# Merge units of the self-attention stage: fixed places in TensorE's order, lower planner rank, part of their vector work on GpSimd

## The chip, the cores and the metric

The kernel runs on one core of a Trainium2 chip. A core has a matrix engine (TensorE; PE in the profile, PEld for its weight loads), a vector engine (VectorE, DVE), a scalar engine (ScalarE, ACT), a general engine (GpSimd, POOL) and SyncE (SP), which here only issues DMAs. The metric is device time in microseconds (us); a median of several runs is given.

## The reference

One inference step of a one-layer encoder over 1024 prompt tokens and 8 x 16 sample tokens (together T = 1152), width 1024, all in float32. The input u is normalised and projected by `w_in`; three branches follow, and their results are merged:

```python
A: o_a = diff_attn(q, k, v) * silu(g_a)        # 8 heads, chunk-causal mask + ALiBi bias
B: o_b = rg_lru(conv(x_r)) * silu(g_b)
C: o_c = cross_attention(q_m, 256 memory tokens) * silu(g_c)
p = einsum('btnw,nwd->btnd', stack([o_a, o_b, o_c]), w_branch)
m = sum_n sigmoid(g_merge_n) * p_n
x = LayerNorm(alpha * x + m @ w_o)

# differential attention, per head: two score matrices over the halves of q and k
s1 = q1 k1^T * scale + bias;  s2 = q2 k2^T * scale + bias
w  = softmax(s1) - lam * softmax(s2)
o  = w @ v;  o = o * rsqrt(mean(o*o) + eps) * subln_g * lam_scale
```

The merge is a matrix product of 1152 x 1024 by 1024 x 1024 for each of the three branches, weighted by a gate and added up.

## The kernel before

**Precision.** Products that need nearly full float32 run as three passes: each operand is split into a high half (a cast on ScalarE, line 134) and a low half (the value minus its high half, on VectorE, line 131); `mm3` issues high x high, high x low, low x high.

**Stages ("windows").** After the projections come `wkg` (recurrent branch B and most of the projections), then `wkc` (cross-attention of the prompt), `wkx` (cross-attention of the samples), `wka` (self-attention of the prompt: this is where most of the change lies, from about 1330 to 1656 us), `wks` (self-attention of the samples), then the output product and the last LayerNorm.

**Merge units.** While an attention stage runs, the merge product of a branch that is already done is used as fill work for TensorE. `m_units(i, e)` gives, for branch i and the block e of 128 output columns, three units, one for each third of the 1152 tokens (384). A unit (`units_for`) loads its gate slice `gmr` (line 271) and, if branches went before, the sum so far `mr` (line 274), both through SP; issues 24 matmuls into a PSUM bank `pj`; then VectorE computes (gate + 1) x product (line 278) and adds the sum so far (line 283); SP stores the result to `d_m` (line 284). The first unit of a block starts the weight load `xr` two blocks ahead; the first two units of a block split the next block's weights in two parts (`w_split`: cast to `xh`, low half to `xl`).

**Self-attention, per head h.** `tload` loads a bias table into `th` (one buffer) and GpSimd scales it for the head (line 313). `qk` makes the high half of the two query halves and the masked copies (`Q`, lines 324 and 325), loads the raw keys and splits them (`K`, lines 134 and 131); Q and K have one buffer each, and the raw keys take the buffers that the raw queries leave. For each block i of 128 queries, `s1` issues the scores `sc` of both halves (i+1 key blocks), VectorE adds the table and takes the minimum (line 366, 16 such instructions a head), ScalarE takes the exponential (line 369), and VectorE combines the two softmaxes (line 376). `s2` transposes the weights (TensorE, line 387; ScalarE copies, line 389), `s3` multiplies by v. The step i of `s1` is followed by `s2` and `s3` of i-2; what is left after `s1` of i = 7 is `tail`: `s2` and `s3` of 6 and 7, `s4a` (the norm; its square root on ScalarE) and `s4b` (transpose, gate, store).

**What sets the order.** Each engine works through its own instruction stream in order. A planner makes the streams when the kernel is built: it follows the program with estimated durations and gives each engine, of the instructions that are ready by its estimate, the one that stands earliest in the program. So a merge unit that stands late in the program is issued early wherever an engine would stand idle. `seq` (lines 426 to 444) is the program order: three units ahead of head 0, then two in each of the 8 heads, the first behind the `s1` of i = 5 with its `s2` and `s3` of 3, the second inside `tail`, which stands behind `qk` of the next head:

```python
seq += at[:18] + [F[2 * h]] + at[18:]
seq += [lambda h=h: (qk(h + 1), tload(h + 1), vload(h + 1))] + tail[:3] + [F[2 * h + 1]] + tail[3:]
```

**Cross-attention of the prompt, start.** `setup` (line 453) loads the 256 x 1024 memory keys with one DMA into `mr`, stores them to an output, and `qget` loads the queries; `mk_tr` transposes the keys by blocks of 256 columns.

## Time and profile before

| | us |
|---|---|
| median of 3 runs | 2013.34 (2007.81 to 2016.94) |
| profiled execution, its own time | 2009.19 |
| its span | 2006.8 |
| TensorE busy | 1929.4 |
| VectorE busy | 1275.0 |
| ScalarE busy | 951.4 |
| GpSimd busy | 118.1 |

Matmuls overlap one another, so a busy TensorE need not be at its peak. The granted clock is a share of TensorE's full speed. The chain that ended last lies for 86% of the span on TensorE, 5% on VectorE, 4% on DMA and 3% on ScalarE. "Idle before" in a row is the time in which the engine stood still ahead of that instruction, with what ended it.

### The profile page before, as it was taken

The numbers are of one execution on the slowest core, as the hardware profiler recorded it, in microseconds if no ns is written. First come the engines' busy times: TensorE is split into PE (matmuls) and PEld (weight loads), VectorE is DVE, ScalarE is ACT, GpSimd is POOL, SyncE is SP. The second block draws the span as 40 slices with busy tenths as digits, with TensorE's granted clock in tenths as the row PEclk, the third lists the DMA queues.
The fourth block names the chain that finished last, engine by engine and source line by source line (L and its number), as shares of the span: only waits on it lengthen the run. The fifth ranks groups of instructions, "written<-read, shape, count | busy, mean of one in ns | idle before, by whom it ended". The sixth has DMA issues, their size and how long they took to land.

```text
span 2006.8 us, 35547 instructions
## 1 busy us (share of the span) xinstructions
PE 1929.4 (96%) x13880; PEld 1792.8 (89%) x13880; DVE 1275.0 (64%) x2402; ACT 951.4 (47%) x2035; POOL 118.1 (6%) x186
## 2 busy tenths in 40 slices
PE   7999999999999999999999899999998778999998
PEld 7999999999999999999999888878997666677986
DVE  7746776655655575756545464459998764444688
ACT  5433333445545555655445432338877763323310
POOL 2100000000000000000000001000110001110000
PEclk9999999999999999999999999999998889999999
DMA  8756333343443343333424856978676418777952
GB/s 272 239 159 178 120 102 111 114 139 126 137 146 118 130 128 118 110 125 122 151 96 147 269 187 219 309 241 248 195 207 176 116 39 266 257 253 247 296 159 94
DMA packets 314151, 344.58 MB, mean 172 GB/s; under 512 B 19124, under 2 KB 262196, under 8 KB 313984
## 3 DMA queue, kind: packets, MB, share of 16 engines
q1 hardware_dynamic: 313984, 342.32, 54.1%
q8 instruction: 109, 1.79, 0.4%
q14 instruction: 58, 0.48, 0.1%
HBM read 241.45 MB, written 100.81 MB: 171 GB/s over the span
## 4 chain that ended last, share of the span: by engine, by line
PE 86%; DVE 5%; DMA 4%; ACT 3%; issue 1%; SPq 1%; POOL 0%; DVEq 0%; ACTq 0%
PE pj L138 23%; PE ba L1026 15%; PE bb L1026 14%; PE bc L1026 14%; PE sc L138 6%; PE o L138 4%; PE tr L387 1%; PE tr L601 1%; PE tr L138 1%; PE pv L138 1%; DMA ocr<-d_oT 1%; PE tr L415 1%; PE tr L743 1%; DVE p L366 1%; DMA d_oT<-oc 1%
## 5 line engine op out<-in xcount | busy, mean ns | idle before, releaser
L138 PE MATMUL pj<-uhi,xh 128*128 128x384 f32 x576 | 200.1, 347 | 0.9 <-DVE gmr L278 0.7
L138 PE MATMUL pj<-ulo,xh 128*128 128x384 f32 x576 | 197.9, 344 | 1.0 <-DVE ulo L131 1.0
L138 PE MATMUL pj<-uhi,xl 128*128 128x384 f32 x576 | 197.5, 343 | 0.0
L134 ACT CAST xh<-xr 128x512 fp32r<-128x512 f32 x124 | 74.4, 621 | 104.5 <-PE pj L138 50.1
L138 PEld LDWEIGHTS pj<-ulo,xh 128*128 128x128 f32 x576 | 108.8, 189 | 10.8 <-issue 8.2
L138 PEld LDWEIGHTS pj<-uhi,xh 128*128 128x128 f32 x576 | 108.8, 189 | 10.7 <-issue 5.8
L138 PE MATMUL sc<-K,Q 128*128 128x512 f32 (+4 forms) x384 | 107.7, 391 | 7.3 <-ACT K L134 2.8
L138 PEld LDWEIGHTS pj<-uhi,xl 128*128 128x128 f32 x576 | 108.7, 189 | 5.3 <-issue 4.6
L369 ACT ACTIVATE p<-p,sst 128x256 f32<-128x256 f32 (+6 forms) x128 | 100.6, 788 | 21.1 <-DVE sst L366 20.4
L138 PE MATMUL pj<-w,uhi 128*128 128x256 f32 x576 | 106.9, 286 | 0.5 <-ACT uhi L134 0.2
L366 DVE CUSTOM_DVE_ANT_0 p<-sc,th 128x256 f32<-128x256 f32 (+6 forms) x128 | 98.3, 769 | 12.7 <-PE sc L138 9.8
L138 PE MATMUL pj<-wo,mh 128*128 128x512 f32 x432 | 98.7, 390 | 0.3 <-ACT wo L134 0.3
L131 DVE TENSOR_TENSOR xh<-s,xh 128x512 fp32r<-128x512 f32 x80 | 55.1, 689 | 66.7 <-ACT xh L134 65.6
L138 PEld LDWEIGHTS pj<-wo,mh 128*128 128x128 f32 x432 | 80.8, 188 | 18.0 <-ACT wo L134 1.0
L131 DVE TENSOR_TENSOR xl<-s,xl 128x512 fp32r<-128x512 f32 x80 | 55.2, 690 | 61.7 <-ACT xl L134 60.5
L138 PEld LDWEIGHTS pj<-w,uhi 128*128 128x128 f32 x576 | 90.8, 193 | 1.6 <-ACT uhi L134 0.7
L1026 PE MATMUL ba<-uhi,xh 128*128 128x288 f32 x432 | 91.0, 296 | 0.4 <-DVE go L1041 0.4
L1026 PE MATMUL ba<-uhi,xl 128*128 128x288 f32 x432 | 90.7, 295 | 0.0
L1026 PE MATMUL bb<-uhi,xl 128*128 128x288 f32 x432 | 90.7, 296 | 0.0
L1026 PE MATMUL bc<-uhi,xh 128*128 128x288 f32 x432 | 90.7, 295 | 0.0
L1026 PE MATMUL bc<-uhi,xl 128*128 128x288 f32 x416 | 87.8, 296 | 0.0
L1026 PE MATMUL bb<-uhi,xh 128*128 128x288 f32 x416 | 87.7, 296 | 0.0
(319 smaller groups left out, 5132.8 us busy)
## 6 DMA issues: line engine op xcount, KB each, us to landing
xr<-in_w_in_dram SPq DMA_DIRECT2D x82, 512.0 KB, 4.8
xr<-in_w_branch_dram SPq DMA_DIRECT2D x32, 512.0 KB, 5.1
ck<-in_cache_k_dram SPq DMA_DIRECT2D x32, 512.0 KB, 6.9
cv<-in_cache_v_dram SPq DMA_DIRECT2D x16, 1024.0 KB, 5.9
d_gm<-go SPq DMA_DIRECT2D x24, 576.0 KB, 3.3
gmr<-d_gm SPq DMA_DIRECT2D x72, 192.0 KB, 4.2
d_m<-gmr SPq DMA_DIRECT2D x64, 192.0 KB, 2.4
mr<-d_m SPq DMA_DIRECT2D x48, 192.0 KB, 4.9
```

Of the source, the lines that this page charges most:

```text
L131: V.tensor_tensor(out, a, b, OP.subtract)
L134: SC.copy(hi, src)
L138: PE.matmul(out, a, b, start=start, stop=stop)
L366: V.tensor_tensor_reduce(s[:, :L].rearrange("p (a b) -> p a b", a=nb), ps[z][:, :nb, :w], X["th"][:, 896 - 128 * i:896 - 128 * i + L].rear ...
L369: SC.activation(s[:, :L], s[:, :L], AF.Exp, scale=-1.0, bias=st_[:, z, i:i + 1], accum_out=st_[:, 2 + z, i:i + 1])
L387: PE.transpose(t[:, 128 * j:128 * j + 128], X["w", h, i][:, 128 * k:128 * k + 128], ident)
L415: PE.transpose(t[:, 128 * j:128 * j + 128], X["ob", h][:, 4 * g + j, :], ident)
L601: PE.transpose(t[:, 128 * j:128 * j + 128], X["ck", n, s // 2][:, j, 128 * (s % 2):128 * (s % 2) + 128], ident)
L743: PE.transpose(t[:, 256 * d + 128 * m:256 * d + 128 * m + 128], X["k", b][:, m, c:c + 128], ident)
L1026: PE.matmul(t, w[:, p, k, :], m[v][:, k, a], start=first and k == 0 and y == 0, stop=last and k == 3 and y == 2, skip_group_check=True)
```

## The change

- The 18 units of branch C in the self-attention stage (`m_units(2, e)`, e = 1 to 6) get `eng=GP`: their sum (line 283) and the weight low halves of the block that follows (`w_split`) move from VectorE to GpSimd.
- `mm` returns its instruction; `s1` keeps the last score matmul in `X["at"]`. `behind(f)` builds a unit within `tc.issue_after`: its TensorE instructions get an ordering edge that puts them behind that matmul in TensorE's stream (an order, not a wait for it to finish). Other engines' instructions get no edge.
- `first(fs)` builds the attention steps `at` and `tail` within `tc.high_priority(100)`: the planner ranks them as if they stood 100 instructions earlier. `qk`, `tload`, `vload`, `gload` and the units are not in it.
- The first unit of a head moves from behind `at[:18]` to behind `at[:15]`, which ends with `s1` of i = 5; the second from behind `tail[:3]` (in the last head `tail[:6]`) to behind `tail[:1]`.
- In `s4a` one 128 x 8 product moves from VectorE to a Square on ScalarE.
- `setup` of the prompt's cross-attention loads the memory keys with four DMAs of 256 columns each.

```diff
-    def split(hi, lo, src):
+    def split(hi, lo, src, eng=None):
         SC.copy(hi, src)
-        sub(lo, src, raw(hi))
+        (eng or V).tensor_tensor(lo, src, raw(hi), OP.subtract)
 
     def mm(out, a, b, start, stop):
-        PE.matmul(out, a, b, start=start, stop=stop)
+        return PE.matmul(out, a, b, start=start, stop=stop)
...
-    def w_split(i, part):
+    def w_split(i, part, eng=None):
...
-        split(wt[i][0][:, a], wt[i][1][:, a], wr[i][:, a])
+        split(wt[i][0][:, a], wt[i][1][:, a], wr[i][:, a], eng)
...
             for p in range(2):
                 if str(p) in do:
-                    w_split(i + 1, p)
+                    w_split(i + 1, p, eng)
...
             if more:
-                V.tensor_tensor(g, x["m"], g, OP.add)
+                (eng or V).tensor_tensor(g, x["m"], g, OP.add)
             SY.dma_start(d_m[e][:, TC * c:TC * c + TC], g)
...
-                        mm(t[:, b, :w], q, X["K"][z][y][:, w * b:w * b + w], y == 0, y == 1)
+                        X["at"] = mm(t[:, b, :w], q, X["K"][z][y][:, w * b:w * b + w], y == 0, y == 1)
...
-            V.scalar_tensor_tensor(d, z1, EPS, z1, op0=OP.mult, op1=OP.mult)
+            SC.activation(d, z1, AF.Square, scale=EPS ** 0.5)
...
         for e in range(1, 7):
-            F += m_units(2, e)
+            F += m_units(2, e, eng=GP)
+
+        def behind(f):
+            def go():
+                with tc.issue_after(X["at"].ins):
+                    f()
+            return go
+
+        def first(fs):
+            def go(f):
+                with tc.high_priority(100):
+                    f()
+            return [lambda f=f: go(f) for f in fs]
...
-            seq += at[:18] + [F[2 * h]] + at[18:]
+            at, tail = first(at), first(tail)
+            seq += at[:15] + [behind(F[2 * h])] + at[15:]
             if h < 7:
-                seq += [lambda h=h: (qk(h + 1), tload(h + 1), vload(h + 1))] + tail[:3] + [F[2 * h + 1]] + tail[3:]
+                seq += [lambda h=h: (qk(h + 1), tload(h + 1), vload(h + 1))] + tail[:1] + [behind(F[2 * h + 1])] + tail[1:]
                 seq.append(lambda h=h: gload(h + 1))
             else:
-                seq += tail[:6] + [F[15]] + tail[6:]
+                seq += tail[:1] + [behind(F[15])] + tail[1:]
...
-            SY.dma_start(mr, d_kv[:, 0:D].rearrange("(a p) d -> p a d", p=128))
+            for j in range(4):
+                c = slice(256 * j, 256 * j + 256)
+                SY.dma_start(mr[:, :, c], d_kv[:, c].rearrange("(a p) d -> p a d", p=128))
```

## Rows read from the trace of the kernel before

**Rows 1.** The page: busy us (share) and instructions; granted clock in 40 slices.
```profile
PE 1929.4 (96%) x13880; PEld 1792.8 (89%) x13880; DVE 1275.0 (64%) x2402; ACT 951.4 (47%) x2035; POOL 118.1 (6%) x186
PEclk9999999999999999999999999999998889999999
```

**Rows 2.** Scaling of the head's table on GpSimd, seven of eight: start, duration, idle before.
```profile
1378.90 4.41 POOL L313 TENSOR_SCALAR th<-th 128x1152 f32<-128x1152 f32 x1 [40.90 <-DMA th<-in_c_tab_dram]
1414.80 4.81 POOL L313 TENSOR_SCALAR th<-th 128x1152 f32<-128x1152 f32 x1 [31.48 <-DMA th<-in_c_tab_dram]
...
1524.80 3.44 POOL L313 TENSOR_SCALAR th<-th 128x1152 f32<-128x1152 f32 x1 [29.79 <-DMA th<-in_c_tab_dram]
1566.11 4.21 POOL L313 TENSOR_SCALAR th<-th 128x1152 f32<-128x1152 f32 x1 [37.87 <-DMA th<-in_c_tab_dram]
1604.84 4.22 POOL L313 TENSOR_SCALAR th<-th 128x1152 f32<-128x1152 f32 x1 [34.52 <-DMA th<-in_c_tab_dram]
```

**Rows 3.** Stretches: length, busy of PE, PEld, DVE, ACT, POOL; clock, DMA share, GB/s.
```profile
1387.10:1410.70 23.60, 23.60 (x149) 21.32 (x149) 22.64 (x66) 20.48 (x56) 0.00 (x0) 1.00 0.72 208
1410.70:1423.30 12.60, 12.60 (x95) 12.16 (x93) 11.37 (x17) 8.63 (x23) 4.81 (x1) 1.00 0.69 190
1576.90:1600.60 23.70, 20.12 (x102) 15.46 (x102) 20.92 (x60) 18.88 (x54) 0.00 (x0) 0.86 0.39 111
1600.60:1614.10 13.50, 9.33 (x63) 8.67 (x63) 7.94 (x14) 9.45 (x23) 4.22 (x1) 0.87 0.44 122
1638.20:1656.10 17.90, 10.58 (x71) 9.33 (x72) 6.74 (x15) 7.20 (x21) 0.00 (x0) 0.84 0.04 15
1660.00:1680.00 20.00, 15.92 (x96) 12.25 (x95) 7.98 (x16) 5.00 (x8) 3.69 (x16) 1.00 1.01 325
```

**Rows 4.** Stretches, instructions on the merge units' bank alone: PE, PEld, DVE, ACT.
```profile
1387.10:1410.70 23.60, 10.93 (x47) 7.94 (x47) 1.08 (x2) 0.00 (x0) 1.00 0.72 208
1410.70:1423.30 12.60, 6.42 (x33) 5.18 (x31) 0.54 (x1) 0.00 (x0) 1.00 0.69 190
1351.20:1524.80 173.60, 76.77 (x351) 59.69 (x349) 8.64 (x16) 0.00 (x0) 1.00 0.75 213
```

**Rows 5.** VectorE in order of time, from one head to the next, with fill.
```profile
1416.54 0.54 DVE L278 SCALAR_TENSOR_TENSOR gmr<-gmr,pj 128x384 f32<-128x384 f32 x1
1417.12 2.67 DVE L283 TENSOR_TENSOR gmr<-mr,gmr 128x384 f32<-128x384 f32 x1
...
1422.06 1.23 DVE L131 TENSOR_TENSOR K<-qr,K 128x1024 fp32r<-128x1024 f32 x1 [1.14 <-ACT K L134]
...
1423.28 0.42 DVE L366 CUSTOM_DVE_ANT_0 p<-sc,th 128x256 f32<-128x256 f32 x1
...
1424.11 0.55 DVE L278 SCALAR_TENSOR_TENSOR gmr<-gmr,pj 128x384 f32<-128x384 f32 x1
```

**Rows 6.** VectorE in order of time, from head 6 to head 7, without fill.
```profile
1612.75 1.23 DVE L131 TENSOR_TENSOR K<-qr,K 128x1024 fp32r<-128x1024 f32 x1 [2.21 <-ACT K L134]
```

**Rows 7.** Groups of VectorE and GpSimd: count, busy us, mean ns, idle before.
```profile
L283 DVE TENSOR_TENSOR gmr<-mr,gmr 128x384 f32<-128x384 f32 x21 | 13.6, 648 | 0.1
L278 DVE SCALAR_TENSOR_TENSOR gmr<-gmr,pj 128x384 f32<-128x384 f32 x21 | 11.4, 543 | 9.0 <-PE pj L138 9.0
L131 DVE TENSOR_TENSOR xl<-xr,xh 128x512 fp32r<-128x512 f32 x14 | 9.4, 681 | 0.0
L955 POOL TENSOR_TENSOR rt<-ra 128x576 f32<-128x576 f32 x16 | 19.2, 1198 | 542.5 <-DVE rc L954 542.5
L1164 POOL TENSOR_TENSOR w<-wr,w 128x512 fp32r<-128x512 f32 x12 | 18.0, 1506 | 53.7 <-ACT w L1162 53.7
```

**Rows 8.** SP's queue: start, issue time, line, transfers.
```profile
1412.22 4.32 SPq L318 DMA_DIRECT2D qr<-d_k  x4
```

**Rows 9.** TensorE and ScalarE, start of the prompt's cross-attention.
```profile
1119.45 0.66 PE L465 MATMUL tr<-ident,mr 128*128 128x128 f32 x4 [3.30 <-DMA mr<-d_kv]
...
1123.19 2.01 ACT L486 ACTIVATE qm<-qr 128x1024 fp32r<-128x1024 f32 x2
```

More of the change, by code (lines that the diff above doesn't have):

```diff
@@ L239, in w_split, with units_for @@
         a = slice(4 * part, 4 * part + 4)
-        split(wt[i][0][:, a], wt[i][1][:, a], wr[i][:, a])
+        split(wt[i][0][:, a], wt[i][1][:, a], wr[i][:, a], eng)
     PLANS = {"a": {0: "L"}, "b": {1: "L0", 2: "1"}, "": {0: "L0", 1: "1"}, "s": {2: "L01"}}
-    def units_for(col, ev, w, pre, cs=(0, 1, 2), plan=""):
+    def units_for(col, ev, w, pre, cs=(0, 1, 2), plan="", eng=None):
         i = len(order)
@@ L264, in body, with m_units @@
     gq_ = [None]
-    def m_units(i, e, put=None, cs=(0, 1, 2), plan=""):
+    def m_units(i, e, put=None, cs=(0, 1, 2), plan="", eng=None):
         x = {}
@@ L282, in ev @@
             if more:
-                V.tensor_tensor(g, x["m"], g, OP.add)
+                (eng or V).tensor_tensor(g, x["m"], g, OP.add)
             SY.dma_start(d_m[e][:, TC * c:TC * c + TC], g)
-        return units_for(128 * e, ev, w_br[i], pre, cs, plan)
+        return units_for(128 * e, ev, w_br[i], pre, cs, plan, eng)
     def swap(wk, i, ps, bufs):
```

## The prediction

> **What bounds the kernel now.** The page comes first: TensorE is busy for 96% of the span at full clock, except in the 31st to 33rd of 40 slices, where the granted clock falls [rows 1]. A slice is 50.2 us, so the fall lies near 1505 to 1656 us: the second half of the self-attention stage. Everything else that the change touches there is read from this stage, not from the 96%.
>
> The stage has a clock of its own: the table scaled on GpSimd once a head. From 1378.90 to 1524.80 four heads pass, 36.5 us each; the next two take 41.3 and 38.7 us, and the last needs 51.3 us from its scaling at 1604.84 to the end of the stage at 1656.1 [rows 2, 3]. So heads got slower although nothing was added to them. The stretches say why. A head falls into a score phase (from the first to the last of the sixteen line-366 instructions) and a boundary (from there to the first of the next head). [...] The merge units make the difference: 16 of them (the line-278 count) ran between 1351.2 and 1524.8 in 76.77 us of TensorE, 4.8 us each, about 3.3 a head [rows 4]. The program places two a head; the planner spent them early, and the last three heads had none.
>
> The early and the bare heads differ by only 2 to 5 us, so TensorE is not the only bound. Without units an early head holds 23.60 - 10.93 = 12.7 us of TensorE in its score phase and 12.60 - 6.42 = 6.2 us in the boundary [rows 3, 4]. VectorE holds 20.9 us in the bare score phase of 23.7 [rows 3]: nearly the phase. The boundary is a chain: the last scores free Q, ScalarE and VectorE make the next Q, that frees the buffers for the raw keys, their DMAs go out at 1412.22 [rows 8], ScalarE casts, VectorE makes the low half at 1422.06, and the next line 366 starts at 1423.28, as that ends [rows 5]. The low half waited 1.14 us for ScalarE; in a bare boundary 2.21 [rows 5, 6].
>
> **The change part by part.** *Units behind given scores.* Two a head, 2 x 4.8 = 9.6 us of TensorE, one in the score phase and one in the boundary. TensorE then holds 12.7 + 4.8 = 17.5 us in the score phase and 6.2 + 4.8 = 11.0 in the boundary, below both lengths. The edge orders one engine's stream and adds no wait at run time; queued behind a unit are attention matmuls, and the lower rank lets ready ones go between. The clock: 51% of a bare head is real TensorE work at full clock ((12.7 + 6.2) / 37.2), and there it falls; at (17.5 + 11.0) / 35.2 = 81% I take 1.00, as the stretch at 1660 us had with 15.92 of 20 us busy [rows 3]. If it falls there too, the phase goes back to the bare 23.7.
>
> *Score phase.* VectorE's bare 20.9, plus one line 278 of 0.54 [rows 7], plus port waits (below) 0.4, plus the 1.0 us that it idled in a filled phase (23.60 - 22.64, [rows 3]): 22.9 us. Bounds: 21.9 with no idle time, 23.7 as now.
>
> *Boundary.* 12.6 with fill; one low half of 0.68 [rows 7] leaves VectorE's queue ahead of Q, port waits add 0.4: 12.3 us. Bounds: 11.9, and 13.5 as in a bare one [rows 3]. The lower rank of `qk` against `tail` puts copies of `tail` ahead of Q and K on ScalarE; that cost is inside the upper bound, since ScalarE already makes the key's low half wait 2.21 there [rows 6]. A head: 35.2 us, bounds 33.8 to 37.2.
>
> *Work moved to GpSimd.* A head loses two sums of 0.65 and 1.33 low halves of 0.68 on VectorE, 2.2 us [rows 7]. On GpSimd no row shows these shapes in this stage; the nearest are 1.51 us for a 128x512 low half and 1.20 for a 128x576 product, which by size gives 0.80 for a sum [rows 7]: 2 x 0.80 + 1.33 x 1.51 = 3.6 us a head. GpSimd has room, 4.81 of 36 us being used [rows 2]. But the two engines disturb each other: the sum at 1417.12 took 2.67 us instead of 0.65, and ended at 1419.79, just after GpSimd's table scaling (1414.80 + 4.81 = 1419.61) [rows 2, 5]. So a VectorE operation with two operands from SBUF can wait for a GpSimd operation that has begun. The wait is between nothing and the whole 3.6 us; I take 0.8 a head (0.4 in each part), nearer the lower end, since at these durations most starts miss each other.
> [...]
>
> *Queues passed.* The store of a unit now waits on SP for GpSimd instead of VectorE. Behind it stand the raw keys of the next head if the planner puts them there: 0 to 4.81 us (one table scaling, [rows 2]); I take 0, since the keys go out at 1412.22 and the boundary's unit is only read at 1416.54 [rows 5, 8]. On POOL the table scaling can stand behind a unit's sum: the second rival below the forecast.
>
> *Small edits.* The Square takes one 128x8 instruction from VectorE to ScalarE, out of 60 or more in a phase: 0, within 0.2 us either way. The memory keys in four pieces: TensorE waited 3.30 us for the whole load [rows 9] and can start a transpose on the first quarter, but the scores behind need the queries, which ScalarE only converts at 1123.19 [rows 9], and three more DMA issues stand ahead of the queries' load. Bounds -3.3 and +3.2 (three issues at 4.32/4 = 1.1, [rows 8]); I take -1, a third of the wait, as the queries come late anyway.
>
> *Sum.* The four early heads: 4 x (36.5 - 35.2) = 5.2. The two bare ones: 41.3 + 38.7 - 70.4 = 9.6. The last: score phase 23.7 to 22.9, and its end of 17.9 at clock 0.84 [rows 3] to some 16 at full clock: 2.7. Start of head 0: 0, its load on VectorE being the least. Keys: 1. Together 18.5; 2009.19 - 18.5 = 1990.7, so **1991 us**. The profiled execution lies 4.2 below the median and inside the runs shown, so I leave the number as it is.
>
> **Rivals.** *Full overlap (1973 us).* If the chains hide, the head is set by the busiest engine: VectorE 20.9 + 7.9 + 1.1 = 29.9, TensorE 28.5 [rows 3, 4], with 10% of waits 33 us. That gives 4 x 3.5 + (80 - 66) + 7 for the last head (the mean gain of a bare one) + 1 = 36. For it: every engine is then near 30. Against it: the boundary's DMA chain is not touched.
> *Port (2013 us, no change).* GpSimd's 3.6 us a head all fall on VectorE's path: 2.8 more than taken, times 8 is 22. For it: the 2.67. Against it: only some VectorE operations read two SBUF operands; line 278, whose product is in PSUM, took its 0.54 us at 1416.54 in the midst of the scaling [rows 2, 5].
> *Table behind the sum (2026 us, slower).* Place: POOL's in-order stream in the boundary. The scaling ends at 1419.61, 3.7 us before the line 366 that needs it [rows 2, 5]. If the sum of the boundary's unit stands ahead of it, the scaling starts only when that unit is done. It decides from the point where the unit's line 278 starts later than 1423.28 - 4.81 - 0.80 - 0.54 = 1417.1; today two start at 1416.54 and 1424.11 [rows 5], one on each side. At 1424.11 the table would be ready at 1430.3, 7 us late; 5 us, between on time and that, over 7 boundaries is 35 against the gain: 1991 + 35 = 2026. Against it: the planner would have to expect the unit earlier than the table's DMA.
>
> **How the numbers follow.** What a measurement of this kernel can tell from no change is about 0.5%, 10 us: faster is below 2003. Forecast 0.52, own range 1979 (head 33.8) to 2008 (head 37.2): 0.45 faster, 0.07 same. Full overlap 0.13, faster. Port 0.19: 0.02 faster, 0.14 same, 0.03 slower. Table 0.16: 0.04 same, 0.12 slower. So faster 0.60, same 0.25, slower 0.15. The range 1970 to 2018 leaves out the far end of the full overlap and most of the table's case.
>
> **What would show it.** Right: line-278 instructions come two a head to the end of the stage; the granted clock stays near 1.00 from 1520 to 1640; the eight scalings lie 34 to 36 us apart. Wrong: scalings 37 us or more apart with the clock at 1.00 (the chain or the port); line 376 or the key's low half well above their durations (port); a table scaling that waits for a merge sum, and line 366 for it (table); the clock falling in each boundary.

## The result, and the profile after

The changed kernel takes 2032.99 us (median of 6 runs, 2028.46 to 2038.63) against 2013.96 for the kernel before in the same runs (6 runs, 2007.81 to 2021.10): a ratio of 1.0097 (95% interval 1.0069 to 1.0125). It is slower, by 19 us; 18.5 us of gain were forecast, and the time lies outside the range. (Every ratio below is against the kernel before on the same chip in the same rounds of runs; it is not made from the medians and can differ a little from theirs.)

The profiled execution took 2032.9 us, its span is 2031.1, 24.3 us longer than that of before, whose execution was one of the quicker ones. The page of the changed kernel, the lines that answer to [rows 1]:

```profile
PE 1937.6 (95%) x13880; PEld 1799.9 (89%) x13880; DVE 1272.8 (63%) x2364; ACT 954.2 (47%) x2043; POOL 148.7 (7%) x216
...
PEclk9999999999999999999999899989898998999999
```

Four things that the change was to do, it did. The 18 sums and 12 low halves ran on GpSimd (its busy time rose by 30.6 us). Units came two a head up to the end of the stage (line-278 counts 1, 2, 2, 2, 2, 2, 2, 3 from head 0 to head 7; before 3, 3, 4, 3, 3, 0, 0, 0). The clock no longer falls in one block of slices, but a little in many. And the heads became even. They became evenly slow: GpSimd's scaling of the table, to be held against [rows 2], now three of the eight.

```profile
1424.73 3.27 POOL L313 TENSOR_SCALAR th<-th 128x1152 f32<-128x1152 f32 x1 [22.20 <-DMA th<-in_c_tab_dram]
...
1466.50 3.57 POOL L313 TENSOR_SCALAR th<-th 128x1152 f32<-128x1152 f32 x1 [22.66 <-DMA th<-in_c_tab_dram]
...
1505.35 3.72 POOL L313 TENSOR_SCALAR th<-th 128x1152 f32<-128x1152 f32 x1 [23.29 <-DMA th<-in_c_tab_dram]
```

From the second scaling to the last (1386.84 to 1625.34) a head takes 39.75 us; from 1378.90 to 1604.84 it took 37.66 before [rows 2].

**Where the 24.3 us came in**, read by landmarks of the two traces. The first scores of the stage start 4.2 us later (1349.4 to 1353.6). The last line 366 pair of head 0 is 7.5 late. Over the next seven heads 14.8 more come in, 2.1 a head, and that pair of head 7 is 22.2 late. The end of the stage is 21.4 late, and the first transpose of the next window 25.0 (1670.4 to 1695.4). From there on the lag stays. So some 15 of the 24 us are the length of heads 1 to 7, about 3 more that of head 0, and the rest lies ahead of the first scores and behind the last head.

**Which part of a head grew.** The prediction's boundary between heads (first line 366 of a head) is no good mark any more: block 0's scores now start before the second key is ready, so that "boundary" shrank from 12.6 to 9.1 us while the "score phase" grew from 23.6 to 29.9 or 33.0. A mark that holds in both kernels is the start of line 366 for block i = 3, where all of K, the table and the buffers of the head before are there. From block 3 to block 7 (the *late part*) a head took 12.7 us before and takes 14.9 now; from block 7 to block 3 of the next head (the *turn*) 25.1 before, 24.9 now (means of seven). Stretches of before and then of after, with the columns of [rows 3]: the late part and the turn of one head, and the seven heads as a whole.

```profile
1432.20:1444.90 12.70, 12.70 (x84) 12.02 (x83) 11.65 (x32) 10.69 (x33) 0.00 (x0) 1.00 0.81 241
1444.90:1469.40 24.50, 24.26 (x168) 22.75 (x166) 21.81 (x51) 18.90 (x46) 4.55 (x1) 1.00 0.70 189
1371.52:1635.60 264.08, 240.93 (x1476) 213.14 (x1475) 227.25 (x524) 203.46 (x532) 32.10 (x7) 0.92 0.60 169
```

```profile
1444.00:1460.00 16.00, 15.18 (x78) 13.61 (x79) 12.77 (x31) 12.22 (x35) 0.00 (x0) 0.81 0.45 132
1460.00:1483.90 23.90, 20.05 (x137) 17.51 (x135) 19.21 (x39) 16.32 (x42) 5.58 (x3) 1.00 0.65 175
1378.97:1657.84 278.87, 244.23 (x1481) 215.67 (x1480) 220.87 (x491) 204.10 (x541) 52.31 (x31) 0.93 0.54 153
```

Over the seven heads the clock hardly moved (0.92 to 0.93) and VectorE was busy 6.4 us less, as the offload should make it; the stretch is 14.8 us longer all the same. No engine is full: TensorE 88%, VectorE 79%, ScalarE 73%. What grew is waiting. TensorE and VectorE of the changed kernel at the start of a late part:

```profile
1483.57 0.33 PE L387 MATMUL tr<-ident,p 128*128 128x128 f32 x1 [0.84 <-DVE ost L417]
1484.26 0.79 PE L138 MATMUL o<-v,wT 128*128 128x128 f32 x2 [0.35 <-ACT wT L389]
1484.70 2.00 PE L138 MATMUL sc<-K,Q 128*128 128x512 f32 x5
...
1490.34 0.94 PE L138 MATMUL o<-v,wT 128*128 128x128 f32 x6 [0.57 <-ACT wT L389]
1491.03 1.14 PE L138 MATMUL sc<-K,Q 128*128 128x384 f32 x5
```

```profile
1485.94 0.69 DVE L366 CUSTOM_DVE_ANT_0 p<-sc,th 128x512 f32<-128x512 f32 x1 [0.83 <-PE sc L138]
...
1487.43 0.82 DVE L366 CUSTOM_DVE_ANT_0 p<-sc,th 128x640 f32<-128x640 f32 x1 [0.79 <-PE sc L138]
```

TensorE waits for a copy of ScalarE or for VectorE, with the scores behind in its queue, and VectorE waits for those scores: over the seven heads line 366 waited 15.0 us for them, before 9.6. At the end of the late part VectorE has another instruction between the last two blocks. Before, then after:

```profile
1515.16 1.07 DVE L366 CUSTOM_DVE_ANT_0 p<-sc,th 128x896 f32<-128x896 f32 x1
...
1516.46 1.02 DVE L376 SCALAR_TENSOR_TENSOR p<-p,cc,p 128x768 f32<-128x768 f32 x1
...
1518.27 1.23 DVE L366 CUSTOM_DVE_ANT_0 p<-sc,th 128x1024 f32<-128x1024 f32 x1 [0.29 <-PE sc L138]
```

```profile
1495.37 1.09 DVE L366 CUSTOM_DVE_ANT_0 p<-sc,th 128x896 f32<-128x896 f32 x1
...
1496.38 1.01 DVE L376 SCALAR_TENSOR_TENSOR p<-p,cc,p 128x768 f32<-128x768 f32 x1
1497.73 1.22 DVE L325 SCALAR_TENSOR_TENSOR Q<-qr,Q 64x1024 fp32r<-64x1024 f32 x1 [0.34 <-ACT Q L324]
1498.99 1.23 DVE L366 CUSTOM_DVE_ANT_0 p<-sc,th 128x1024 f32<-128x1024 f32 x1
```

The extra one, line 325, is the low half of the next head's query, ahead of block 7's line 366. From block 6 to block 7 there are 5.6 us in the mean, 3.8 before.

### The profile page after: what moved, and what is told of

Read it like the earlier page. It is cut to its first block, busy times and chain, and to the rows that moved or that the text cites. A ratio compares the mean times of both kernels' runs of the same rounds, so it can differ in the third digit from the quotient of the medians.

```text
span 2031.1 us, 35558 instructions
## 1 busy us (share of the span) xinstructions
PE 1937.6 (95%) x13880; PEld 1799.9 (89%) x13880; DVE 1272.8 (63%) x2364; ACT 954.2 (47%) x2043; POOL 148.7 (7%) x216
## 4 chain that ended last, share of the span: by engine, by line
PE 83%; DVE 6%; DMA 4%; ACT 3%; issue 2%; SPq 1%; POOL 1%; DVEq 0%; ACTq 0%; POOLq 0%
PE pj L138 21%; PE ba L1042 14%; PE bb L1042 14%; PE bc L1042 14%; PE sc L138 6%; PE o L138 5%; PE tr L617 1%; PE tr L387 1%; PE tr L138 1%; PE pv L138 1%; DVE K L135 1%; DMA ocr<-d_oT 1%; DVE w L1180 1%; DVE ost L417 1%; PE tr L642 1%
## 5 line engine op out<-in xcount | busy, mean ns | idle before, releaser
L138 PE MATMUL sc<-K,Q 128*128 128x512 f32 (+4 forms) x384 | 115.0, 408 | 20.8 <-DVE K L135 10.7
L366 DVE CUSTOM_DVE_ANT_0 p<-sc,th 128x256 f32<-128x256 f32 (+6 forms) x128 | 97.5, 773 | 27.3 <-PE sc L138 18.5
L138 PE MATMUL o<-v,wT 128*128 128x128 f32 x576 | 97.2, 298 | 11.6 <-ACT wT L389 7.4
L138 PEld LDWEIGHTS o<-v,wT 128*128 128x128 f32 x576 | 84.2, 206 | 22.9 <-ACT wT L389 13.8
L138 PEld LDWEIGHTS sc<-K,Q 128*128 128x128 f32 x384 | 73.7, 218 | 29.9 <-DVE K L135 12.3
```

What stands on the lines that cost most here:

```text
L138: return PE.matmul(out, a, b, start=start, stop=stop)
L366: V.tensor_tensor_reduce(s[:, :L].rearrange("p (a b) -> p a b", a=nb), ps[z][:, :nb, :w], X["th"][:, 896 - 128 * i:896 - 128 * i + L].rear ...
```

## The experiments

Three theories stood at the start. *GpSimd*, the rival "port": a GpSimd instruction that has begun blocks one of VectorE's, as the sum that took 2.67 us instead of 0.65 [rows 5, 7]. *Rank*: the attention steps' higher rank puts `tail` ahead of the next head's queries and keys. *Edge*: a unit's 24 matmuls stand in TensorE's queue ahead of attention matmuls. "Head" below is the mean of the seven spacings of block 7, "late" and "turn" its two parts as above, "clock" the granted clock over those seven heads. All are read from each kernel's trace, which is one execution: that of before took 2009.19 us, one of the quicker of its kernel, that of e4 2018.31, the slowest of ten. So differences of less than about 1 us a head say little by themselves, and the ratio decides.

| kernel | us | ratio, 95% | head | late | turn | clock |
|---|---|---|---|---|---|---|
| before | | 1 | 37.7 | 12.7 | 25.1 | 0.92 |
| changed | 2032.99 | 1.0097 (1.0069-1.0125) | 39.8 | 14.9 | 24.9 | 0.93 |
| e1 no GpSimd | 2039.26 | 1.0129 (1.0104-1.0154) | 40.0 | 15.1 | 24.8 | 0.93 |
| e2 no rank | 2051.87 | 1.0202 (1.0168-1.0237) | 42.4 | 16.1 | 26.3 | 0.88 |
| e3 no edge | 2039.80 | 1.0127 (1.0098-1.0155) | 40.9 | 14.5 | 26.4 | 0.93 |
| e4 GpSimd only | 2009.89 | 0.9979 (0.9961-0.9997) | 38.5 | 13.1 | 25.4 | 0.90 |
| e5 small edits only | 2018.69 | 1.0016 (1.0001-1.0031) | 38.3 | 12.5 | 25.8 | 0.94 |
| e6 rank only | 2026.06 | 1.0048 (1.0032-1.0065) | 39.9 | 16.3 | 23.6 | 0.94 |
| e7 edge only | 2061.67 | 1.0221 (1.0187-1.0256) | 44.1 | 17.3 | 26.7 | 0.86 |
| e8 thin units | 2050.18 | 1.0159 (1.0131-1.0188) | 43.0 | 15.3 | 27.7 | 0.85 |
| e9 loose edge | 2017.34 | 1.0023 (1.0009-1.0038) | 37.8 | 13.5 | 24.3 | 0.97 |
| e10 loose edge, rank | 2029.87 | 1.0085 (1.0068-1.0102) | 39.7 | 13.2 | 26.5 | 0.93 |
| e11 query late | 2048.93 | 1.0179 (1.0163-1.0196) | 41.7 | 13.5 | 28.2 | 0.92 |
| e12 spread | 2021.25 | 1.0039 (1.0025-1.0053) | 38.4 | 15.2 | 23.2 | 0.99 |
| e13 rank, scores | 2081.24 | 1.0335 (1.0301-1.0369) | 45.8 | 24.0 | 21.7 | 0.88 |
| e14 rank, tail | 2046.42 | 1.0154 (1.0126-1.0182) | 41.2 | 16.1 | 25.1 | 0.89 |
| e15 rank, all | 2047.35 | 1.0163 (1.0127-1.0199) | 40.9 | 16.0 | 24.9 | 0.92 |
| e16 spread early | 2017.22 | 1.0010 (0.9993-1.0026) | 37.8 | 12.4 | 25.4 | 0.96 |
| e17 one piece later | 2018.49 | 1.0029 (1.0016-1.0042) | 38.0 | 12.6 | 25.4 | 0.96 |
| e18 query casts first | 2022.17 | 1.0042 (1.0025-1.0059) | 38.7 | 13.8 | 24.9 | 0.97 |

### One part taken out, and one alone (e1 to e4)

```diff
# e1: changed kernel, sums and low halves on VectorE
-            F += m_units(2, e, eng=GP)
+            F += m_units(2, e)
# e2: changed kernel without the rank
-            at, tail = first(at), first(tail)
# e3: changed kernel without the edge (all three places)
-            seq += at[:15] + [behind(F[2 * h])] + at[15:]
+            seq += at[:15] + [F[2 * h]] + at[15:]
# e4: kernel before with GpSimd's part alone
-            F += m_units(2, e)
+            F += m_units(2, e, eng=GP)
```

> The changed kernel with the merge sums and the weight low halves back on VectorE (edge, rank, places, Square and the four key loads stay). [...] Theory rank (the attention steps ahead of the next head's Q and K in the planner's rank put the second key cast behind the tail on ScalarE, 11 us after the last line 366): stays at 2028 to 2036. Theory edge (a unit that may not run ahead leaves TensorE idle and its clock falling in the middle of a score phase): stays at 2028 to 2036.

> The changed kernel with the attention steps at their own rank (no 100 places ahead); edge, places and GpSimd stay. Theory rank: 2005 to 2015 us, the second key cast comes some 7 to 10 us after the last line 366 instead of 11. Theory GpSimd and theory edge: stays within 5 us of 2033.

> The changed kernel without the ordering edge: units stand at the new places but may be issued wherever TensorE is free; rank and GpSimd stay. Theory edge: 2010 to 2018 us, line 278 comes three a head again in the early heads and the early heads are back near 36.5 us. Theory rank and theory GpSimd: stays within 5 us of 2033.

> The kernel before with only the merge sums and the weight low halves of the 18 units on GpSimd. Theory GpSimd: 2022 to 2032 us, with the key's low half well above 1.23 us. Theory rank and theory edge: 2008 to 2016, no change.

No part taken out brings the time back, and without the rank it is clearly worse. GpSimd's part is the only one that seems to pay: 0.9979 alone, its interval just below 1; without it the changed kernel is at 1.0129 instead of 1.0097 (those two intervals overlap). So the work moved to GpSimd is not what made the kernel slower. The blocking itself is there: in the changed kernel the first key's low half, 1.23 us in [rows 5], took 3.51 beside the scaling of 1505.35 (1505.35 + 3.72 = 1509.07), with TensorE, and the tail's matmuls in its queue, behind it.

```profile
1506.40 3.51 DVE L135 TENSOR_TENSOR K<-qr,K 128x1024 fp32r<-128x1024 f32 x1 [0.32 <-ACT K L134]
```

```profile
1509.96 0.39 PE L138 MATMUL sc<-K,Q 128*128 128x256 f32 x1 [1.95 <-DVE K L135]
```

So the rows show the blocking, and the times a small gain all the same.

Nor did the blocking as a whole make it slower; in the changed kernel nearly all of it comes from the table's scaling, which is on GpSimd in every kernel. Take what each of VectorE's instructions took beyond the median of the same instruction in all these kernels, where that is over 0.1 us: over the seven heads it adds up to 13.1 us in the changed kernel and 10.1 before, but only to 7.9 in e6 and 4.9 in e10 (below), whose heads are as long as the changed kernel's. And in the changed kernel the five turns in which a key's low half was blocked took 24.9 us in the mean, the two others 24.8 and 25.3.

### Each ordering part alone (e5 to e7)

```diff
# e5: kernel before + new places, Square, four key loads
+            seq += at[:15] + [F[2 * h]] + at[15:]
+            ... tail[:1] + [F[2 * h + 1]] + tail[1:]
# e6: kernel before + rank alone, old places
+            at, tail = first(at), first(tail)
# e7: kernel before + edge alone, old places
+            seq += at[:18] + [behind(F[2 * h])] + at[18:]
+            ... tail[:3] + [behind(F[2 * h + 1])] + tail[3:]
```

> The kernel before with the new places of the units in the program, the Square on ScalarE and the keys in four loads; no edge, no rank, merge sums on VectorE. This is what the three kernels with one part taken out still had in common. Theory A (what they have in common costs): about 2035 us, the stage's heads near 39 us. Theory B (edge and rank each cost by themselves, by what they do to the order of the attention): 2005 to 2018, no change that can be told; the last heads bare as before. B is held likelier, 2 to 1.

> The kernel before with the higher rank of the attention steps alone (units at their old places, no edge, no GpSimd, no Square, one key load). Theory B: slower, 2022 to 2040, because qk stands behind the copies of tail on ScalarE, so that the second key's cast comes 2 to 4 us later in each of seven heads (14 to 28 us). Theory A: 2014, no change. If the rank only keeps units from being spent early, the last heads are filled, and the time falls to about 1995.

> The kernel before with the ordering edge alone, at the old places and with no rank. Theory B: 2030 to 2050, as the kernel without the rank had (2051.87 us): the units come two a head but then stand ahead of attention matmuls in TensorE's order. Theory A: about 2014.

This parts them. The small edits are worth nothing that can be told. The rank alone costs 2.2 us a head by the two traces (12 us in all by the medians), the edge alone 6.3. The edge's cost can be seen whole in e7: VectorE has done block 5, TensorE works through the unit, and block 6's scores come behind it. TensorE (from the first to the last `pj` row there are 20 of the unit's 24 matmuls, and eight `o` matmuls of the attention), then VectorE:

```profile
1454.74 0.43 PE L138 MATMUL pj<-ulo,xh 128*128 128x384 f32 x1
...
1459.29 0.33 PE L138 MATMUL pj<-uhi,xl 128*128 128x384 f32 x1
1459.46 1.81 PE L138 MATMUL sc<-K,Q 128*128 128x448 f32 x8
```

```profile
1453.99 0.96 DVE L366 CUSTOM_DVE_ANT_0 p<-sc,th 128x768 f32<-128x768 f32 x1
...
1460.72 1.08 DVE L366 CUSTOM_DVE_ANT_0 p<-sc,th 128x896 f32<-128x896 f32 x1
```

From block 5 to block 6 e7 takes 8.6 us in the mean, before 3.7: 4.9 more, the length of a unit. With the rank added (the changed kernel) this gap is 3.1, so the rank does let the scores go ahead of the unit; it pays elsewhere. (The other 1.6 us of e7's head lie in the turn. There the second query's low half took 3.9 us instead of 1.2 in six of seven heads, beside the table's scaling.)

In the heads the changed kernel is as long as the rank alone makes it (39.8 and 39.9). It is slower than e6 (their intervals just miss each other) in two other places: from the first scores to block 7 of head 0 it takes 25.4 us and e6 21.7, and behind the last head 17.9 and 14.0 (taken up under "The end of the stage").

### Is it TensorE's time? (e8)

```diff
+                if eng:
+                    mm(t[:, :TC], wt[i][0][:, k, :], uhi[:, k, TC * c:TC * c + TC], k == 0, k == 7)
+                    continue
                 mm3(t[:, :TC], ...)
```

> The changed kernel with one of the three matmul passes of the units of branch C in the self-attention (high x high alone: the low x high and high x low products are left out), so 1.6 us of TensorE a unit instead of 4.8. All other instructions stay. If the units' own TensorE time lengthens the head, up to 2 x 3.2 x 8 = 51 us go: 1982 to 2005. If the head is set by the chain of the other engines (key split, tail, weights), the stage stays: 2025 to 2040, heads at 38 us or more with TensorE idle more often. Without the units' work the granted clock may fall more often, which would take some of it back.

A miss for both: with two thirds of the units' matmuls left out the kernel is slower than the changed one. In the heads compared, VectorE's order in the late part is the same, and so nearly is its length (15.3 against 14.9); the turn grew by 2.8 us, and the clock fell from 0.93 to 0.85 over the seven heads:

```profile
1379.77:1680.51 300.74, 229.78 (x1257) 192.56 (x1256) 233.90 (x491) 205.15 (x541) 66.11 (x31) 0.85 0.50 141
```

But VectorE's 491 instructions, as many as in the changed kernel, took 13.0 us more in these heads (233.90 against 220.87), and GpSimd's 31 took 13.8 more. The units end at another place now: their sums come while VectorE does line 376 of blocks 6 and 7, and the table's scaling, behind them, meets the first key's low half in all seven heads. The changed kernel, then e8, where line 376 has become 379:

```profile
L135 DVE TENSOR_TENSOR K<-qr,K 128x1024 fp32r<-128x1024 f32 x14 | 29.1, 2078 | 20.3 <-ACT K L134 20.3
...
L376 DVE SCALAR_TENSOR_TENSOR p<-p,cc,p 128x1024 f32<-128x1024 f32 x7 | 9.0, 1286 | 0.2
...
L376 DVE SCALAR_TENSOR_TENSOR p<-p,cc,p 128x896 f32<-128x896 f32 x7 | 8.1, 1152 | 0.2
```

```profile
L135 DVE TENSOR_TENSOR K<-qr,K 128x1024 fp32r<-128x1024 f32 x14 | 35.9, 2563 | 27.0 <-ACT K L134 27.0
...
L379 DVE SCALAR_TENSOR_TENSOR p<-p,cc,p 128x1024 f32<-128x1024 f32 x7 | 13.6, 1947 | 0.3
L379 DVE SCALAR_TENSOR_TENSOR p<-p,cc,p 128x896 f32<-128x896 f32 x7 | 13.6, 1945 | 0.0
```

These three groups hold all of the 13.0 us, and the seven heads grew by 21.9. So e8 doesn't tell what the units' TensorE time is worth: taking it away also made GpSimd block VectorE for longer and went with a lower clock, and no run here parts these.

### Fill and clock without rank or solid blocks (e9, e10, e12)

```diff
# e9: kernel before + GpSimd, looser edge (s1 keeps X["e", i], the last score of block i)
+            seq += at[:18] + [behind(F[2 * h], 0)] + at[18:]
+            ... tail[:3] + [behind(F[2 * h + 1], 4)] + tail[3:]
# e10: changed kernel with the same looser edges
# e12: kernel before + GpSimd, each unit in four pieces u, v of six matmuls, each with its edge
+            seq += at[:6] + u[:1] + at[6:10] + u[1:2] + at[10:14] + u[2:3] + at[14:18] + u[3:]
+            seq += at[18:22] + v[:1] + at[22:] + v[1:2]
+            ... tail[:3] + v[2:3] + tail[3:6] + v[3:] + tail[6:]
```

> The kernel before with GpSimd's part and a looser edge: the units stand at their old places in the program, without a rank, and a head's two units are held behind the first and the fifth block's scores of that same head, so TensorE can take their matmuls one by one from there on, wherever it is free. Theory F (what costs is that a unit becomes one solid block late in the head; two units a head as free filler would do what the change was meant to do): heads near 37 us to the end of the stage, 1995 to 2005. Rival C (fill is no gain by itself: heads are bound by the order of VectorE and ScalarE, and two units a head instead of three lower the granted clock): 2015 to 2030.

> The changed kernel with the looser edge of the run above (behind the first and the fifth block's scores of the head), rank and all else kept. If the rank's own cost (two scores blocks 1.3 us and more apart because the next head's query low half is put ahead of line 366 on VectorE) is what is left once the blocks are loose: 2020 to 2030. If the fixed late edge was the cost in the changed kernel: near 2000. If edge and rank only cost together by TensorE waiting behind attention matmuls that are not ready: 2025 to 2040.

> The kernel before with GpSimd's part, no rank, and each unit cut into four pieces of six matmuls (1.2 us), each piece behind another block's scores: the first unit's behind those of blocks 2 to 5, the second's behind 6 and 7 and two in the tail. If the solid block of 4.8 us is what the edge costs without a rank (blocks 5 and 6 were 8.6 us apart instead of 3.7): the gap falls to 5 us or less and the time to 2000 to 2020. If any order ahead of attention matmuls costs its whole TensorE time: 2040 to 2060 as before.

e9 does what the change was meant to do: two units in each head, no solid block, the clock up. The seven heads of e9 and of e12:

```profile
1378.20:1642.66 264.46, 235.40 (x1493) 210.45 (x1492) 218.75 (x499) 202.12 (x532) 55.37 (x29) 0.97 0.60 163
```

```profile
1381.92:1650.56 268.64, 235.54 (x1487) 203.36 (x1486) 220.90 (x501) 203.19 (x536) 55.32 (x29) 0.99 0.58 159
```

264.46 us against the 264.08 of before at clock 0.92. Even fill and a nearly full clock are worth nothing that can be told here: the last three heads together gain 3.8 us (117.3 before, 113.5 in e9), and the four before them, which had had three or four units each, lose 4.2 (146.8, 151.0). With the rank (e10) the same loose edges give 39.7, as the changed kernel. So the late place of the edge is not what the changed kernel still pays for: every kernel with the rank on both `at` and `tail` lies at 39.7 us or above, whatever its edges and whichever engine adds (39.7 to 40.9, e11 at 41.7 and e8 at 43.0).

### The query's low half (e11)

```diff
+            with tc.issue_after(X["ttr"].ins) if "ttr" in X else ExitStack():
                 V.scalar_tensor_tensor(q[b], r[b], -1.0, raw(q[b]), op0=OP.mult, op1=OP.subtract)
...
+                X["ttr"] = V.tensor_tensor_reduce(...)   # line 366
```

> The changed kernel with an order on VectorE: the low halves of the next head's queries (line 325) are built behind the last line 366 of the head. In the changed kernel one stands between the last two blocks in every head (1.22 us, blocks 5.6 us apart instead of 3.8). If it lies on the path: the score part of a head falls by 1.2 to 1.8 us, the stage by 9 to 14, 2019 to 2024. If the chain over the keys takes it back: within 4 us of the changed kernel, 2029 to 2037.

Behind the last line 366 the low half costs more: the late part falls by 1.4 us as expected, and the turn rises by 3.3. Most of that is no chain over the keys: the second query's low half now starts just behind the table's scaling in all seven heads and takes 3.9 us instead of 1.2 (VectorE, then GpSimd):

```profile
1429.00 3.91 DVE L326 SCALAR_TENSOR_TENSOR Q<-qr,Q 64x1024 fp32r<-64x1024 f32 x1
```

```profile
1428.58 3.48 POOL L313 TENSOR_SCALAR th<-th 128x1152 f32<-128x1152 f32 x1 [20.74 <-DMA th<-in_c_tab_dram]
```

The 1.22 us between two blocks was the cheaper place; what this place would cost without the scaling beside it wasn't tried.

### Which half of the rank (e13 to e15)

```diff
# e13
-            at, tail = first(at), first(tail)
+            at = first(at)
# e14
+            tail = first(tail)
# e15: changed kernel, queries, keys and loads of the next head ranked too
-                seq += [lambda h=h: (qk(h + 1), tload(h + 1), vload(h + 1))] + ...
+                seq += first([lambda h=h: (qk(h + 1), tload(h + 1), vload(h + 1))]) + ...
```

> The changed kernel with the rank on the score steps (at) alone; the steps of tail have none. If the cost of the rank is that tail gets ahead of the next head's queries and keys: heads fall from 39.8 to about 38, 2012 to 2022. If it is the score steps' own rank: it stays, 2028 to 2038. If the units then come ahead of tail, as without any rank: 2040 or more.

> The changed kernel with the rank on the steps of tail alone. If tail ahead of queries and keys is the rank's cost: heads at 40 us or more, since in the score part the unit's block then also stands ahead of the late scores (8.6 us between two blocks, as with the edge alone): 2040 to 2060. If the score steps' rank is the cost: 2010 to 2025.

> The changed kernel with queries, keys, table load and value load of the next head in the rank as well, so that among the attention's own steps the order is that of the kernel before, and only the units and the gate load rank lower. If the rank costs by tail ahead of queries and keys: heads at 37.7 us or less, 2000 to 2018. If the rank costs since the units no longer go ahead of any attention step: heads stay near 39.8, 2025 to 2038.

The theory that the rank costs by `tail` getting ahead of queries and keys falls: with them ranked alike (e15) a head takes 40.9, not 37.7. Neither half is the harmful one. Without the tail's rank (e13) block 3 to block 4 takes 11.6 us, with the tail's norm and output copies in between, and the head is 45.8; without the scores' rank (e14) the unit's block is back ahead of block 6 (6.9 us there). Why the rank alone costs 2.2 us a head stays open; rank alone with queries and keys in it wasn't tried.

### What a head's length hangs on (e16 to e18)

```diff
# e16: as e12, no piece ahead of the scores of blocks 5 to 7
+            seq += at[:2] + u[:1] + at[2:6] + u[1:2] + at[6:10] + u[2:3] + at[10:14] + u[3:]
+            seq += at[14:] + v[:1]
+            ... tail[:3] + v[1:2] + tail[3:6] + v[2:3] + tail[6:] + v[3:]
# e17: as e12, one piece moved behind block 7's scores
-            seq += at[18:22] + v[:1] + at[22:] + v[1:2]
+            seq += at[18:] + v[:2]
# e18: as e16, the query casts ranked
+            with tc.high_priority(100):
                 SC.activation(q, r, AF.Copy, scale=-1.0)
```

> The kernel before with GpSimd's part, no rank, and the units in four pieces of six matmuls each, none of them between the scores of blocks 5, 6 and 7: the first unit's behind blocks 1 to 4, the second's behind block 7 and in the tail. With the earlier cut the part from block 3 to block 7 took 15.2 us (12.7 before) and the rest 23.2 (25.1). If pieces ahead of late scores cost their time: 13 and 23.5, heads at 36.5, 2000 to 2010. If not: heads at 38 again, 2015 to 2025.

> The kernel with cut units (pieces behind blocks 2 to 7 and in the tail), with one piece moved from behind block 6's scores to behind block 7's; nothing else. If a piece ahead of late scores costs by itself: the gap from block 6 to 7 falls from 6.3 to about 4.5, the rest stays at 23.2, heads at 36.5, 2005 to 2012. If the cost only moves to the other part: heads near 38, 2015 to 2023.

> The kernel with no piece ahead of the late scores, with the higher rank on the two ScalarE casts of the next head's queries (line 324) alone. If the second query's chain sets the rest of the head: its low half ends 3 us after the last line 366 or sooner, the rest falls from 25.4 to 23.5, and if the score part keeps its 12.4 heads are 36 us, 2000 to 2008. If the casts ahead of the last exponentials cost the score part as much: heads near 37.8, 2012 to 2020.

e16 and e17 give the late part back (12.4 and 12.6, from 15.2), so pieces ahead of the late scores do cost their time. But the turn takes it: 25.4 in both, from 23.2. The turns of e16, four of the seven, show what it goes with:

```profile
1378.27:1401.70 23.43, 21.29 (x140) 18.39 (x138) 19.22 (x46) 17.97 (x45) 4.27 (x2) 1.00 0.83 222
1414.10:1439.50 25.40, 22.42 (x139) 19.64 (x137) 19.84 (x44) 18.85 (x46) 8.59 (x4) 0.93 0.64 167
1451.90:1479.40 27.50, 23.43 (x139) 20.76 (x137) 21.50 (x44) 17.79 (x44) 4.12 (x2) 0.88 0.56 149
...
1568.00:1591.40 23.40, 20.80 (x140) 18.16 (x138) 18.56 (x45) 17.95 (x44) 5.16 (x2) 1.00 0.66 176
```

The same program part takes 23.4 us at clock 1.00, 25.4 at 0.93 and 27.5 at 0.88. Two things are mixed in this. In the first, second and fourth of these rows the second query's low half ended 5.2 to 5.3 us after the last line 366, and there the turn differs by 2 us with the clock. In the third it ended 7.9 us after, as in the two other turns of 26 us and more (7.8). That later end is GpSimd's doing. The second and the third of these turns, VectorE and then GpSimd:

```profile
1420.52 1.21 DVE L345 SCALAR_TENSOR_TENSOR Q<-qr,Q 64x1024 fp32r<-64x1024 f32 x1
...
1458.32 3.92 DVE L345 SCALAR_TENSOR_TENSOR Q<-qr,Q 64x1024 fp32r<-64x1024 f32 x1
```

```profile
1420.54 4.18 POOL L333 TENSOR_SCALAR th<-th 128x1152 f32<-128x1152 f32 x1 [12.47 <-DMA th<-in_c_tab_dram]
...
1458.29 3.12 POOL L333 TENSOR_SCALAR th<-th 128x1152 f32<-128x1152 f32 x1 [12.42 <-DMA th<-in_c_tab_dram]
```

Where the low half started 0.02 us ahead of the table's scaling it took 1.21 us, where it started 0.03 us behind, 3.92. In e5 it is the same: four turns with this block took 25.9 to 28.0 us, the three others 23.8 to 24.8. Whether a lower clock makes a turn longer or a longer wait lowers the clock, these rows don't tell, and no run moved the scaling out of the way. Ranking the query casts to bring that half forward (e18) didn't pay: late part 13.8, head 38.7.

No kernel here beats the kernel with GpSimd's part alone (e4), 0.2% below the one before.

## Why the prediction was wrong

**The step that failed** is the length of a head with two units in it, 35.2 us (score phase 22.9, boundary 12.3), and in that sum the price of the lower rank. It was put at no more than 1.2 us a head, inside the bound of the boundary, only for copies of `tail` on ScalarE, and at nothing in the score phase. Alone it costs 2.2 us a head (e6), and there the late part, where I had not looked, is 3.6 us longer; every kernel with it has heads of 39.7 us or more, the changed one 39.8. Why it costs that stays open: ranking the queries and keys too doesn't bring it back (e15), and no run isolates the instruction that is in the way. Nor was the gain there without the rank: two units a head as loose fill give 37.8 (e9), as before.

The paragraph "Units behind given scores" was wrong in a second place, the sentence that the edge "orders one engine's stream and adds no wait at run time". In e7 a unit put ahead of the next scores in TensorE's stream made VectorE wait 4.9 us more between two blocks (8.6 instead of 3.7), and the seven heads took 44 us more. I weighed TensorE's total (17.5 of 22.9 us) against the length, when the question was which instruction stands in front of which. In the changed kernel this cost is not seen: that the rank lets ready matmuls go between was right (3.1 us between blocks 5 and 6), and without the edge (e3) it is no faster.

**The early heads' 36.5 us were taken for a state to be improved on.** They had three or four units each, placed one matmul at a time wherever TensorE was free, and the clock at 1.00; single heads got below them (35.6 in e16), no kernel's mean did. The seven heads take 37.7 to 38.5 in every kernel without rank and without a whole unit as one block, but for e18 (38.7), and with units spent early or evenly and the clock anywhere from 0.90 to 0.99. The gain on the bare heads was real in kind, 3.8 us in e9 where 9.6 was forecast for two of them, and the early heads, with fewer units, paid for it; the forecast had these faster by 1.3 each.

**The clock.** I took 1.00; the rows gave 0.93 over the seven heads. That two units a head keep it up held only in kernels without rank on the steps and without whole blocks (0.96 to 0.99 in e9, e12, e16, e17 and e18), and none of these is faster than the kernel before.

**GpSimd.** The sum of 0.80 us came out at 1.08 and the low half of 1.51 at 1.48:

```profile
L283 POOL TENSOR_TENSOR gmr<-mr,gmr 128x384 f32<-128x384 f32 x18 | 19.3, 1077 | 96.6 <-DVE gmr L278 63.5 <-issue 29.1 <-DMA gmr<-d_gm 3.9
L135 POOL TENSOR_TENSOR xl<-xr,xh 128x512 fp32r<-128x512 f32 x12 | 17.5, 1482 | 0.1
```

The offload as a whole doesn't lose (e4, e1), so the rival "port" is not what happened, though its sign came: the first key's low half took 3.5 us or more in five heads, beside the table's scaling. Over the seven heads VectorE's blocked time rose by 3.0 us (10.1 to 13.1), 0.4 a head where 0.8 was taken. No run shows a port behind these "port waits"; the runs show VectorE's instructions taking longer beside GpSimd's, that low half 3.50 to 3.75 us instead of 1.23. Nor is "table behind the sum", the rival on the slower side: line 366 waited for the table twice in the stage, 5.1 us in all, against the 35 of that rival. The slower outcome came by a mechanism that was not among the rivals.

**SP's queue, taken at 0.** At head 0 two stores of units stand ahead of the first keys. SP's queue and TensorE of the changed kernel:

```profile
1343.07 4.67 SPq L284 DMA_DIRECT2D d_m<-gmr  x2
1347.90 1.09 SPq L318 DMA_DIRECT2D qr<-d_k  x2
```

```profile
1353.58 0.58 PE L138 MATMUL sc<-K,Q 128*128 128x256 f32 x1 [7.37 <-ACT K L134]
```

This is about the bound of 4.81 that I had named, and about the 4.2 us by which the stage starts late. But 1.9 of the 4.2 were there before the stage: the last matmul of the samples' cross-attention (`o`) starts at 1331.6, before at 1329.7. From it to the first scores there are 22.0 us in the changed kernel, 19.7 before, 20.9 without GpSimd's part (e1), 20.4 with it alone (e4). So GpSimd's sums can have cost about 1 us here, and that isn't parted from chance. The first scores came late in nearly every variant (1349.2 to 1360.2, before 1349.4); up to 5.6 us of that were there ahead of the stage (1335.3 in e4), where these kernels differ from before in the key loads at most.

**Keys in four pieces.** The first transpose came 2.0 us earlier and the first scores of that stage 0.3 (1124.8 to 1124.5): 0 instead of the 1 us taken, within the bounds. **The end of the stage**, which the sum left out, cost 3.6: from the last line 417 to the next window's first transpose there are 17.9 us instead of 14.3. Where head 7 has three line-278 counts, one unit more than its two, this gap is 14.7 to 18.6 (the changed kernel, e1, e11, e13 and e15), where it has two or none, 13.9 to 15.5. That fits a unit left over behind the stage, but the ranges overlap, and no run took it away alone.

## What to carry to other kernels

Before moving fill work to a fixed place in an engine's queue, ask what stands right behind it and who waits for that (in e7 it was VectorE, 4.9 us more between two blocks); an engine's total against the stage's length doesn't answer it. Where a planner already spends fill one instruction at a time, its early, uneven spending can be as good as an even one: compare the mean over all heads, not the worst head with the best. Look also at which instructions of two engines that block each other start at about the same time: here 0.05 us decided over 2.7 (e16). Mark a loop by an event that both kernels reach in the same state, or a part that only starts earlier will look like one that grew.

## What the runs showed of the hardware

In the changed kernel VectorE's low half of a key, 1.23 us alone, took 3.51 when GpSimd's table scaling had begun before it (1506.40 against 1505.35). In e16 that of a query took 3.92 us where it started 0.03 us behind the scaling, and 1.21 where it started 0.02 us ahead. Where they were blocked in e16 and e5, the turns were the longest (26.0 to 27.5 us in e16, the others 23.4 to 25.4; 25.9 to 28.0 in e5, the others 23.8 to 24.8); in the changed kernel they were not (24.9 in the mean, the others 24.8 and 25.3). Taking TensorE work away (e8) made the kernel no faster: over the seven heads TensorE was busy 14.5 us less than in the changed kernel (244.23 to 229.78), at a granted clock of 0.85 instead of 0.93, and they took 21.9 us more (278.87 to 300.74). VectorE's instructions were 13.0 us longer beside GpSimd there, so the loss isn't shown to be the clock's.
